# A third k-tile pair in seven-product form in block 2's first FFN product, and two of eight pairs in block 1's gate/up products

## The chip, the core and the metric

The kernel runs on one core of a Trainium2 chip. The metric is the device time of one execution in microseconds (us). Before the change three runs took 2608.23, 2606.01 and 2612.13 us; their median is 2608.23.

## The reference, cut to what matters

Two transformer blocks follow each other on 256 tokens of width 2048, all in float32. The change touches one product of each.

```python
# block 1, w_ffn_in: 2048 x 11264, FFN_HIDDEN = 5632
h = rms_norm(x, ffn_pre_g[l])
gate, up = jnp.split(h @ w_ffn_in[l], 2, axis=-1)
x = x + rms_norm((jax.nn.silu(gate) * up) @ w_ffn_out[l], ffn_post_g[l])
...
# block 2, w_ff1: 2048 x 8192
f = jnp.square(jax.nn.relu(x @ w_ff1[layer])) @ w_ff2[layer]
x = layer_norm(DEEPNORM_ALPHA * x + f, ln_ff_g[layer], ln_ff_b[layer])
```

## The kernel before, in words

**Split operands.** Each float32 operand is split into a high part `h` (a rounded copy, ScalarE, L233) and a low part `l` (operand minus `h`, VectorE, L234). A product is three matmuls on TensorE: high by high, high by low, low by high. The tokens stay as the stationary operand (two blocks of 128 tokens, `tb` 0 and 1); the weights move, 512 columns at a time, and each result of 128 tokens x 512 columns fills one PSUM bank.

**The weight stream.** `Stream` loads the weights from HBM in the order of use, in halves of 128 x 1024 (512 KB) on SyncE's queue, into five buffers. Each half becomes one unit (`h` and `l`, five buffers of each). `half()` (L265) hands out a unit and splits ahead until four later units are issued; a unit's split can start only when TensorE is done with the unit five places earlier.

**Normal and seven-product pairs.** k runs over 16 tiles of 128, taken as eight pairs. For 256 tokens x 1024 columns a normal pair (N in `SEQ`) costs two halves, each used by 12 matmuls: 24 matmuls. In seven-product form (S; Strassen's scheme in Winograd's variant) the pair is a 2 x 2 block product: two k-tiles, two token blocks, two column blocks of 512. Seven products instead of eight, so 21 matmuls. VectorE forms the sums of the weights from the two raw halves `a` and `b`: `s` (L254, L255) and `t` (L257, L258), and `splitting4` (L240) makes four units of them, used by 6, 6, 6 and 3 matmuls. The sums of the tokens are formed once by `seven_gen` (L548) and lie in the tile `seven`.

**`seven` (L569).** It runs the eight pairs for one group of 1024 columns. The four results are accumulated in `c[tb, nb]`; products that several results share go to four more banks `m[1]`, `m[5]`, `m[6]`, `m[7]`, over all S pairs of the group. After the last S pair VectorE combines the `m` (L622 to L628, ScalarE copies one, L621), and after the last pair it adds the `c` (L632). With four `c` and four `m`, all eight PSUM banks are in use: the pool `pa` has three, `pb` five.

**Block 2's FFN (`ff2`, L1886)** works the 8192 hidden columns in eight parts of 1024: `i0 i1 o0 i2 o1 ...` (`FF_ORDER`), where `i` is the first product and `o` the second. `i0` is in plain form by `rowsmm` (L457); `i1` to `i7` call `seven` with `SEQ = "NSNNSNNN"`, two S pairs of eight. **Block 1's FFN (`ffn`, L1648)** works 5632 hidden columns in parts of 8, 8, 8, 8, 4 and 8 tiles of 128; all its gate/up products (`i0` to `i5`) are plain `rowsmm`: 512 gate columns, then the 512 up columns that belong to them, evacuated by `ev_glu` (L1677: ScalarE applies Silu, VectorE multiplies).

**What sets the order.** Each engine's program is in the order in which this code emits it. Work that follows a product is pushed with `later` and emitted by `settle`, one step after each half. So a finished 128 x 512 block of hidden values is transposed on TensorE (four 128 x 128 transposes into a bank of `pb`, L1701 in `turn_later`), and one step later the result is split out of PSUM (ScalarE L642, then VectorE L643). Before the first S pair of a group, `seven` empties that list (`while self.late: self.settle()`) and only then takes the four `m` banks, since no bank is left for a transpose.

Of the kernel before, what the change touches and what calls it, by code (L numbers as in the profile page):

```python
# [11 lines left out]
F32R = mybir.dt.float32r  # L12
# [3 lines left out]
AF = mybir.ActivationFunctionType  # L16
# [6 lines left out]
S = 256  # L23
# [15 lines left out]
SEQ = "NSNNSNNN"  # L39
# [21 lines left out]
def _seven(w):  # L61


    u = []
    for p, s in enumerate(SEQ):
        t = w[256 * p:256 * p + 256].reshape(2, 128, 2, 512)
        if s == "N":
            u.append(t.transpose(1, 2, 0, 3).reshape(128, 2048))
        else:
            u.append(np.stack([t[0, :, 1], t[0, :, 0], t[1, :, 0], t[1, :, 1]], axis=1).reshape(128, 2048))  # L70
    return np.stack(u)


def _fours():

    parts = [16 * i for i, s in enumerate(FF_ORDER) if s[0] == "i" and s != "i0"]
    return [i + 2 * p - 16 * len(FF_ORDER) for i in parts for p, s in enumerate(SEQ) if s == "S"]


def _weights(a):  # L80
# [15 lines left out]
    for step in FFN_ORDER:  # L96
        p = int(step[1:])
        lo, hi = int(starts[p]), int(starts[p + 1])
        u.append(gate_up[lo // 4:hi // 4].reshape(-1, 128, 2048) if step[0] == "i" else _rows(w_fo[lo * 128:hi * 128]))
# [11 lines left out]
    for step in FF_ORDER:  # L111
        p = int(step[1:])
        lo, hi = int(starts[p]), int(starts[p + 1])
        if step[0] == "o":
            u.append(_rows(w2[lo * 128:hi * 128]))
        else:
            u.append((_seven if p else _rows)(w1[:, lo * 128:hi * 128]))
# [57 lines left out]
class Stream:  # L175
# [64 lines left out]
    def splitting4(self, j, raw, part):  # L240


        nc = self.nc
        h, l = (self.hp.tile([128, 1024], F32R, tag=x, name=f"{x}{j}") for x in ("h", "l"))
        if part == 0:
            a, b = self.loaded.pop(raw), self.loaded.pop(raw + 1)
            s, t = self.t4([128, 1024], "s"), self.t4([128, 1024], "t")
            self.four = a, b, s, t
        a, b, s, t = self.four
        lo, hi = slice(0, 512), slice(512, 1024)  # L250
        v, n = (b, s, t, a[:, hi])[part], 512 if part == 3 else 1024
        nc.scalar.activation(out=h[:, :n], in_=v, func=AF.Copy)
        if part == 0:
            nc.vector.tensor_tensor(s[:, lo], a[:, hi], a[:, lo], OP.subtract)  # L254
# [4 lines left out]
        nc.vector.tensor_tensor(l[:, :n], v, h[:, :n].bitcast(F32), OP.subtract)  # L259
        if part == 3:  # L260
            self.four = None
        self.done[j] = (h, l)
        self.ns += 1
# [40 lines left out]
class Prog:  # L304
# [152 lines left out]
    def rowsmm(self, xp, nkt, ncb, evac, chain=None, lead=7, lag=0, begin=None):  # L457
# [15 lines left out]
        def run(cb, k2, hl, tb, part=(0, 1)):  # L473
            two = chain and (cb, tb) == (ncb - 1, 1)
            if k2 == 0 and part[0] == 0:
                ps[cb, tb] = (self.acc(), self.bank()) if two else (self.acc(),)
# [71 lines left out]
    def seven_gen(self, xp, box):  # L548
# [3 lines left out]
        ps = [p for p, s in enumerate(SEQ) if s == "S"]  # L552
        t = self.slot([128, len(ps), 2, 4, 128], "seven", F32R)
        for i, p in enumerate(ps):
            yield 1.9
            w = self.t4([128, 2, 4, 128], "s7")
# [9 lines left out]
            self.split2(s, t[:, i, 0], t[:, i, 1])  # L566
        box.append(t)

    def seven(self, xp, st, out, own, more):  # L569
# [4 lines left out]
        last = len(SEQ) - 1  # L574
        last_s = SEQ.rindex("S")
# [15 lines left out]
        for p, s in enumerate(SEQ):  # L591
# [13 lines left out]
            sum_ = lambda i: (st[:, si, 0, i], st[:, si, 1, i])  # L605
# [1042 lines left out]
    def ffn(self):  # L1648
# [6 lines left out]
        ss = self.cp.tile([128, 2, 8], F32, tag="ss", name="ss2")  # L1655
        last = len(FFN_PARTS) - 1
        for step in FFN_ORDER:
            p = int(step[1:])
            nt = FFN_PARTS[p]
            if step[0] == "i":  # L1660
                hid[p] = Pair(self, "hid", nt)
                self.rowsmm(hT, 16, nt // 2, self.ev_glu(hid[p]), lag=4 if p == 0 else 0)
                continue
# [11 lines left out]
            self.rowsmm(hid.pop(p), nt, 4, ev)  # L1675
# [210 lines left out]
    def ff2(self):  # L1886
# [6 lines left out]
        for step in FF_ORDER:  # L1893
            p = int(step[1:])
            nt = FF_PARTS[p]
            if step[0] == "i":
# [11 lines left out]
                if p == 0:  # L1908
                    self.rowsmm(hT, 16, nt // 4, ev, lag=4, begin=lambda: sg.append(self.start(self.seven_gen(hT, st))))
                    continue  # L1910
# [9 lines left out]
                self.seven(hT, st[0], relu2, [self.bank] * 4, [self.acc] * 3 + [self.bank])  # L1920
# [79 lines left out]
```

## Time and profile before

| | |
|---|---|
| median of three runs | 2608.23 us |
| the profiled execution | 2606.45 us, span 2604.7 us |
| TensorE busy / weight load | 99% / 84% of the span |
| VectorE busy | 63% |
| ScalarE busy | 49% |
| granted TensorE clock, mean | 0.996 |
| HBM | 188 GB/s over the span |

Busy time of TensorE is that of overlapping matmuls: a matmul is shown from its start to its modelled end, and the next one starts before that end. The distance of two starts is the time that one more matmul takes. In a row of the timeline the columns are start (us), duration (us), engine, line, operation, output and inputs; a bracket holds the idle time before it and what ended it. In a row of a group, after the bar, stand total busy time (us), mean duration (ns) and the idle time of the engine just before.

### The profile page before, as it was taken

How to read it: one execution, taken by the hardware profiler on the slowest of the kernel's cores; microseconds unless marked ns; L12 is line 12 of the kernel's file. 1: busy time of each engine (PE TensorE's matmuls, PEld its weight loads, DVE VectorE, ACT ScalarE, POOL GpSimd, SP SyncE). 2: the span in 40 equal slices, each digit the busy share in tenths (PEclk: the TensorE clock that was granted, in tenths of full speed). 3: DMA queues.
4: the chain of work that ended last, by engine and by line, in shares of the span. 5: the costliest groups of instructions: out<-in, count | busy, mean ns of one | idle time of the engine just before them, and what ended most of it. 6: DMA issues, size and time to landing. Idle time of an engine off the chain costs nothing. (4 is left out here: it accounts for less than half of the span.)

```text
span 2604.7 us, 33758 instructions
## 1 busy us (share of the span) xinstructions
PE 2574.6 (99%) x13011; PEld 2183.2 (84%) x13011; DVE 1634.4 (63%) x2069; ACT 1281.0 (49%) x1715; POOL 62.4 (2%) x59
## 2 busy tenths in 40 slices
PE   9999999999999999999999999999999999999998
PEld 8999888988888888888888888888788888888886
DVE  5776857766454555554676774456676666676666
ACT  6544666655444444434444464444455545554553
POOL 0000000110000000000010000000100000000001
PEclk9999999999999999999999999999999999999999
DMA  7544557545555555555555655565455555656563
GB/s 282 178 156 146 178 178 244 195 168 187 194 186 194 187 193 188 193 193 190 183 184 188 206 178 179 193 224 185 150 186 198 196 195 179 200 196 209 193 204 121
DMA packets 134081, 493.33 MB, mean 189 GB/s; under 512 B 15149, under 2 KB 15541, under 8 KB 131744
## 3 DMA queue, kind: packets, MB, share of 16 engines
q1 hardware_dynamic: 129888, 470.34, 54.6%
q0 software_dynamic: 2880, 17.76, 2.1%
q10 hardware_dynamic: 1152, 3.07, 0.3%
q8 instruction: 102, 1.67, 0.3%
q14 instruction: 59, 0.48, 0.1%
HBM read 486.91 MB, written 2.11 MB: 188 GB/s over the span
## 5 line engine op out<-in xcount | busy, mean ns | idle before, releaser
L234 DVE TENSOR_TENSOR l<-w,h 128x1024 fp32r<-128x1024 f32 (+1 forms) x852 | 1038.0, 1223 | 857.1 <-ACT h L233 852.5
L233 ACT ACTIVATE h<-w 128x1024 fp32r<-128x1024 f32 (+1 forms) x855 | 898.6, 1057 | 913.0 <-PE pa L488 715.4
L486 PE MATMUL pa<-h,hid 128*128 128x512 f32 (+1 forms) x864 | 338.5, 392 | 0.0
L488 PE MATMUL pa<-h,hid 128*128 128x512 f32 (+1 forms) x864 | 335.0, 388 | 0.0
L487 PE MATMUL pa<-l,hid 128*128 128x512 f32 (+1 forms) x864 | 334.4, 387 | 0.0
L487 PE MATMUL pa<-l,hT 128*128 128x512 f32 x748 | 291.7, 390 | 2.3 <-DVE l L234 2.3
L486 PE MATMUL pa<-h,hT 128*128 128x512 f32 x748 | 293.4, 392 | 0.0
L488 PE MATMUL pa<-h,hT 128*128 128x512 f32 x748 | 291.7, 390 | 0.0
L486 PE MATMUL pa<-h,xT 128*128 128x512 f32 x500 | 201.0, 402 | 2.5 <-ACT ghg L912 1.3
L488 PE MATMUL pa<-h,xT 128*128 128x512 f32 x500 | 195.3, 391 | 0.0
L487 PE MATMUL pa<-l,xT 128*128 128x512 f32 x500 | 194.9, 390 | 0.0
L488 PEld LDWEIGHTS pa<-h,hid 128*128 128x128 f32 x864 | 162.2, 188 | 33.7
L487 PEld LDWEIGHTS pa<-l,hid 128*128 128x128 f32 x864 | 162.4, 188 | 32.2
L486 PEld LDWEIGHTS pa<-h,hid 128*128 128x128 f32 x864 | 162.3, 188 | 31.8
L487 PEld LDWEIGHTS pa<-l,hT 128*128 128x128 f32 x748 | 140.8, 188 | 31.6 <-DVE l L234 2.9
L488 PEld LDWEIGHTS pa<-h,hT 128*128 128x128 f32 x748 | 140.7, 188 | 29.4
L486 PEld LDWEIGHTS pa<-h,hT 128*128 128x128 f32 x748 | 140.7, 188 | 28.6
L583 PE MATMUL pb<-h,hT 128*128 128x512 f32 x378 | 147.1, 389 | 0.0
L585 PE MATMUL pb<-h,hT 128*128 128x512 f32 x378 | 147.1, 389 | 0.0
L584 PE MATMUL pb<-l,hT 128*128 128x512 f32 x378 | 147.0, 389 | 0.0
L443 PE MATMUL pa<-xT,h 128*128 128x256 f32 x496 | 143.2, 289 | 2.3 <-ACT xT L662 2.3
L444 PE MATMUL pa<-xT,h 128*128 128x256 f32 x496 | 141.3, 285 | 0.0
(493 smaller groups left out, 3971.3 us busy)
## 6 DMA issues: line engine op xcount, KB each, us to landing
w<-W SPq DMA_DIRECT2D x889, 512.0 KB, 3.3
row<-rows POOLq DMA_DIRECT2D x7, 1024.0 KB, 7.3
xn<-x ACTq DMA_DIRECT2D x2, 1024.0 KB, 10.2
mn<-mem POOLq DMA_DIRECT2D x2, 1024.0 KB, 7.4
memraw<-memT POOLq DMA_DIRECT2D x2, 1024.0 KB, 6.7
x<-x POOLq DMA_DIRECT2D x2, 1024.0 KB, 7.5
xraw<-xT SPq DMA_DIRECT2D x3, 512.0 KB, 9.8
out<-x SPq DMA_DIRECT2D x6, 256.0 KB, 2.5
```

The lines of the kernel that those rows point to most:

```text
L233: nc.scalar.activation(out=h[:, s], in_=t[:, s], func=AF.Copy)
L234: (nc.gpsimd if j in self.slow else nc.vector).tensor_tensor(l[:, s], t[:, s], h[:, s].bitcast(F32), OP.subtract)
L443: mm(o, h[:, k], xp.H(kt), start=kt == 0, stop=False)
L444: mm(o, h[:, k], xp.L(kt), start=False, stop=False)
L486: mm(o, xh, h[:, k, c], start=kt == 0, stop=False)
L487: mm(o, xh, l[:, k, c], start=False, stop=False)
L488: mm(o, xl, h[:, k, c], start=False, stop=kt == nkt - 1)
L583: mm(o, ah, wh, start=first, stop=False)
L584: mm(o, ah, wl, start=False, stop=False)
L585: mm(o, al, wh, start=False, stop=end)
```

## The change

Block 2's `i1` to `i7` use `SEQ_FF = "NSNSNSNN"`: three S pairs instead of two. Block 1's `i1` to `i5` are computed by `seven` too, with `SEQ_GLU = "NSNNSNNN"`: for each 512 gate columns and the 512 up columns that belong to them one call, nb = 0 being gate and nb = 1 up; two calls in parts of eight tiles, one in the part of four, nine in all. A second call of a part takes its banks the other way round (`swap`): `c` in three banks of `pa` and one of `pb`, `m` in four of `pb`, and the `o` part behind it starts in `pb`. The new `glu` does what `ev_glu` did, from SBUF. The order inside an S pair changes: `m[1]` comes first and `c[0,0]` last, with the weights laid out for it, and `s` is one VectorE operation on 1024 columns with a repeated operand, where two worked on 512 each. `seven_gen` now also runs in block 1's `i0`, and makes its tile for two pairs at a time.

```diff
-SEQ = "NSNNSNNN"
+SEQ_GLU = "NSNNSNNN"
+SEQ_FF = "NSNSNSNN"
...
-            u.append(np.stack([t[0, :, 1], t[0, :, 0], t[1, :, 0], t[1, :, 1]], axis=1).reshape(128, 2048))
+            u.append(np.stack([t[0, :, 0], t[1, :, 1], t[0, :, 1], t[1, :, 0]], axis=1).reshape(128, 2048))
...
-        v, n = (b, s, t, a[:, hi])[part], 512 if part == 3 else 1024
+        v, n = (a, s, t, b[:, hi])[part], 512 if part == 3 else 1024
         nc.scalar.activation(out=h[:, :n], in_=v, func=AF.Copy)
         if part == 0:
-            nc.vector.tensor_tensor(s[:, lo], a[:, hi], a[:, lo], OP.subtract)
-            nc.vector.tensor_tensor(s[:, hi], b[:, hi], a[:, lo], OP.subtract)
+            two = lambda v: v.rearrange("p (i c) -> p i c", i=2)
+            nc.vector.tensor_tensor(two(s), two(a), b[:, lo][:, None].to_broadcast([128, 2, 512]), OP.subtract)
         if part == 1:
-            nc.vector.tensor_tensor(t[:, lo], b[:, hi], s[:, lo], OP.add)
-            nc.vector.tensor_tensor(t[:, hi], b[:, lo], t[:, lo], OP.subtract)
+            nc.vector.tensor_tensor(t[:, lo], a[:, hi], s[:, lo], OP.add)
+            nc.vector.tensor_tensor(t[:, hi], b[:, hi], t[:, lo], OP.subtract)
...
+        own, more = [self.bank] * 4, [self.acc] * 3 + [self.bank]
+        if swap:
+            own, more = more, own
         c = {(tb, nb): own[2 * tb + nb]() for tb in range(2) for nb in range(2)}
...
-            for pair in (((c[0, 0], tok(k0 + 1, 0)), (c[0, 1], sum_(3))), ((m[5], sum_(0)), (m[7], sum_(2))),
-                         ((m[6], sum_(1)), (c[1, 0], tok(k0 + 1, 1))), ((m[1], tok(k0, 0)),)):
+            for pair in (((m[1], tok(k0, 0)), (c[0, 1], sum_(3))), ((m[5], sum_(0)), (m[7], sum_(2))),
+                         ((m[6], sum_(1)), (c[1, 0], tok(k0 + 1, 1))), ((c[0, 0], tok(k0 + 1, 0)),)):
...
-                self.rowsmm(hT, 16, nt // 2, self.ev_glu(hid[p]), lag=4 if p == 0 else 0)
+                if p == 0:
+                    self.rowsmm(hT, 16, nt // 2, self.ev_glu(hid[p]), lag=4, begin=lambda: sv.append(self.start(self.seven_gen(hT, SEQ_GLU, st))))
+                    continue
+                self.drain(sv[0])
+                for b in range(nt // 4):
+                    self.seven(hT, SEQ_GLU, st, self.glu(hid[p], b), swap=b % 2 == 1)
+                after_swap = nt == 8
...
+    def glu(self, hp, b):
...
+        def out(i, tb, nb, t):
+            r = self.rxx[:, tb:tb + 1]
+
+            def f():
+                if nb == 0:
+                    sg[tb] = t
+                    nc.scalar.activation(out=t, in_=t, func=AF.Silu, scale=r)
+                    return
+                nc.vector.scalar_tensor_tensor(out=t, in0=t, scalar=r, in1=sg[tb], op0=OP.mult, op1=OP.mult)
+                self.turn_later(t, hp, 4 * b, tb)
+            self.wait_later(i // 2, f)
```

Three places show what this does to the engines' programs. The first is TensorE at the first S pair of block 2's `i1`. Before, two transposes of `i0`'s last hidden values (`sq` into banks of `pb`) are followed by `c[0,0]` (pb_858) and `c[0,1]` (pb_859):

```order
L1701 MATMUL pb_862_16138<-ident_258,sq_854_16094 128x128 [waits DVE_49,PE_49]
L1701 MATMUL pb_862_16138<-ident_258,sq_854_16094 128x128 x3
L1701 MATMUL pb_863_16145<-ident_258,sq_855_16096 128x128 [waits DVE_49]
L1701 MATMUL pb_863_16145<-ident_258,sq_855_16096 128x128 x3
L583 MATMUL pb_858_16100<-h652_16056,hT20_798_14975 128x512 [waits Activation_49]
L584 MATMUL pb_858_16100<-l652_16057,hT20_798_14975 128x512
L585 MATMUL pb_858_16100<-h652_16056,hT20_798_14975 128x512
L583 MATMUL pb_859_16101<-h652_16056,seven_843_15835 128x512
```

In the change the same place reads as follows, with `m[1]` (pb_962) first:

```order
L1750 MATMUL pb_957_16478<-ident_258,sq_949_16434 128x128 [waits DVE_49,PE_49]
L1750 MATMUL pb_957_16478<-ident_258,sq_949_16434 128x128 x3
L1750 MATMUL pb_958_16485<-ident_258,sq_950_16436 128x128 [waits DVE_49]
L1750 MATMUL pb_958_16485<-ident_258,sq_950_16436 128x128 x3
L606 MATMUL pb_962_16495<-h688_16395,hT20_891_15307 128x512 [waits DVE_49]
L607 MATMUL pb_962_16495<-l688_16396,hT20_891_15307 128x512
L608 MATMUL pb_962_16495<-h688_16395,hT20_891_15307 128x512
L606 MATMUL pb_954_16441<-h688_16395,seven_936_16185 128x512
```

The matmul behind the transposes now waits for VectorE: `m[1]` takes the one bank of `pb` that the second transpose has just filled, the other four being held by `c`. Before, `m[1]` took that bank as well, but was the last of the pair's seven products.

The second place is TensorE between the first and the second 512 gate columns of block 1's `i1`. Before, the second transpose (`sg_440`) stands one half, 12 matmuls, behind the first, ahead of the next half of a plain product:

```order
L486 MATMUL pa_444_6931<-h225_6864,hT0_374_5644 128x512
L487 MATMUL pa_444_6931<-l225_6865,hT0_374_5644 128x512
L488 MATMUL pa_444_6931<-h225_6864,hT0_374_5644 128x512
L1701 MATMUL pb_446_6963<-ident_258,sg_440_6768 128x128 [waits DVE_49]
L1701 MATMUL pb_446_6963<-ident_258,sg_440_6768 128x128 x3
L486 MATMUL pa_443_6924<-h226_6882,hT4_375_5645 128x512 [waits Activation_49]
```

In the change both transposes stand together after the second call's first N pair, and its first S pair follows:

```order
L608 MATMUL pb_461_6972<-h229_6910,hT0_374_5644 128x512
L1750 MATMUL pb_462_7007<-ident_258,u4_454_6847 128x128 [waits DVE_49]
L1750 MATMUL pb_462_7007<-ident_258,u4_454_6847 128x128 x3
L1750 MATMUL pb_463_7016<-ident_258,u5_455_6848 128x128 [waits DVE_49]
L1750 MATMUL pb_463_7016<-ident_258,u5_455_6848 128x128 x3
L606 MATMUL pb_467_7026<-h230_6928,hT0_374_5644 128x512 [waits Activation_49]
L607 MATMUL pb_467_7026<-l230_6929,hT0_374_5644 128x512
L608 MATMUL pb_467_7026<-h230_6928,hT0_374_5644 128x512
L606 MATMUL pa_459_6970<-h230_6928,seven_421_6086 128x512
```

Here `m[1]` (pb_467) waits for its weights alone; it takes a bank that an addition on `c` has freed. The banks of the two transposes go to `m[7]` and `m[6]`, a few products later.

The third place is VectorE at the second S pair of a part of block 2. Before, the four units of the pair have two operations for `s`, two for `t` and four for `l`:

```order
L254 TENSOR_TENSOR s_898_16880<-w690_16831 128x512
L255 TENSOR_TENSOR s_898_16880<-w691_16843,w690_16831 128x512
L259 TENSOR_TENSOR l696_16879<-w691_16843,h696_16878 128x1024
L257 TENSOR_TENSOR t_899_16881<-w691_16843,s_898_16880 128x512
L258 TENSOR_TENSOR t_899_16881<-w691_16843,t_899_16881 128x512
L259 TENSOR_TENSOR l697_16899<-s_898_16880,h697_16898 128x1024
L259 TENSOR_TENSOR l698_16917<-t_899_16881,h698_16916 128x1024
L259 TENSOR_TENSOR l699_16933<-w690_16831,h699_16932 128x512
```

In the change `s` is one operation, and two plain units later the next S pair begins:

```order
L279 TENSOR_TENSOR l732_17206<-w688_17094,h732_17205 128x1024
L277 TENSOR_TENSOR t_996_17208<-w688_17094,s_995_17207 128x512
L278 TENSOR_TENSOR t_996_17208<-w689_17177,t_996_17208 128x512
L279 TENSOR_TENSOR l733_17219<-s_995_17207,h733_17218 128x1024
L279 TENSOR_TENSOR l734_17228<-t_996_17208,h734_17227 128x1024
L279 TENSOR_TENSOR l735_17244<-w689_17177,h735_17243 128x512
L254 TENSOR_TENSOR l736_17264<-w690_17179,h736_17263 128x1024
L254 TENSOR_TENSOR l737_17276<-w691_17191,h737_17275 128x1024
L275 TENSOR_TENSOR s_997_17289<-w692_17203,w693_17259 128x1024
```

Between two S pairs VectorE now has two plain units (l736, l737) where it had four.

More of the change, by code (lines that the diff above doesn't have):

```diff
@@ L69, in _seven @@
         else:
[L70 removed]
+            u.append(np.stack([t[0, :, 0], t[1, :, 1], t[0, :, 1], t[1, :, 0]], axis=1).reshape(128, 2048))
     return np.stack(u)
 def _fours():
[L76 to L77 removed]
+    at = lambda i, seq: [i + 2 * p for p, s in enumerate(seq) if s == "S"]
+    u, n = [], 0
+    for step in FFN_ORDER:
+        nt = FFN_PARTS[int(step[1:])]
+        if step[0] == "i" and step != "i0":
+            for b in range(nt // 4):
+                u += at(n + 16 * b, SEQ_GLU)
+        n += 4 * nt if step[0] == "i" else 2 * nt
+    n += MID
+    for step in FF_ORDER:
+        if step[0] == "i" and step != "i0":
+            u += at(n, SEQ_FF)
+        n += 16
+    return [i - n for i in u]
 def _weights(a):
@@ L98, in _weights @@
         lo, hi = int(starts[p]), int(starts[p + 1])
-        u.append(gate_up[lo // 4:hi // 4].reshape(-1, 128, 2048) if step[0] == "i" else _rows(w_fo[lo * 128:hi * 128]))
+        if step[0] == "o":
+            u.append(_rows(w_fo[lo * 128:hi * 128]))
+        elif p == 0:
+            u.append(gate_up[lo // 4:hi // 4].reshape(-1, 128, 2048))
+        else:
+            for b in range(lo * 128, hi * 128, 512):
+                u.append(_seven(np.concatenate([w_fi[:, i + b:i + b + 512] for i in (0, FFN)], axis=1), SEQ_GLU))
     u += [
@@ L455, in cols, with rowsmm @@
         assert not held
-    def rowsmm(self, xp, nkt, ncb, evac, chain=None, lead=7, lag=0, begin=None):
+    def rowsmm(self, xp, nkt, ncb, evac, chain=None, lead=7, lag=0, begin=None, swap=False):
         mm = self.nc.tensor.matmul
@@ L475, in run @@
             if k2 == 0 and part[0] == 0:
-                ps[cb, tb] = (self.acc(), self.bank()) if two else (self.acc(),)
+                ps[cb, tb] = (self.acc(), self.bank()) if two else ((self.bank if swap and cb == 0 else self.acc)(),)
             h, l = hl
@@ L546, in rowsmm, with seven_gen @@
             chain.after[tb]()
-    def seven_gen(self, xp, box):
+    def seven_gen(self, xp, seq, st):
         nc = self.nc
-        ps = [p for p, s in enumerate(SEQ) if s == "S"]
-        t = self.slot([128, len(ps), 2, 4, 128], "seven", F32R)
-        for i, p in enumerate(ps):
+        for i, p in enumerate(p for p, s in enumerate(seq) if s == "S"):
             yield 1.9
+            if i % 2 == 0:
+                t = self.slot([128, 2, 2, 4, 128], "seven", F32R)
             w = self.t4([128, 2, 4, 128], "s7")
@@ L565, in seven_gen, with seven @@
             yield 0.7
-            self.split2(s, t[:, i, 0], t[:, i, 1])
-        box.append(t)
-    def seven(self, xp, st, out, own, more):
+            self.split2(s, t[:, i % 2, 0], t[:, i % 2, 1])
+            st.append(t[:, i % 2])
+    def seven(self, xp, seq, st, out, swap=False):
         nc, mm, stream = self.nc, self.nc.tensor.matmul, self.stream
-        last = len(SEQ) - 1
-        last_s = SEQ.rindex("S")
+        last = len(seq) - 1
+        last_s = seq.rindex("S")
+        own, more = [self.bank] * 4, [self.acc] * 3 + [self.bank]
+        if swap:
+            own, more = more, own
         c = {(tb, nb): own[2 * tb + nb]() for tb in range(2) for nb in range(2)}
@@ L590, in seven @@
         si = 0
-        for p, s in enumerate(SEQ):
+        for p, s in enumerate(seq):
             if s == "N":
@@ L1674, in ev @@
                     nc.vector.tensor_tensor(c, ps, c, OP.add)
-            self.rowsmm(hid.pop(p), nt, 4, ev)
+            self.rowsmm(hid.pop(p), nt, 4, ev, swap=after_swap)
+            after_swap = False
+    def glu(self, hp, b):
+        nc = self.nc
+        sg = {}
+        def out(i, tb, nb, t):
[8 more added lines that the diff above has]
+            self.wait_later(i // 2, f)
+        return out
     def ev_glu(self, hp):
@@ L1908, in ff2 @@
                 if p == 0:
-                    self.rowsmm(hT, 16, nt // 4, ev, lag=4, begin=lambda: sg.append(self.start(self.seven_gen(hT, st))))
+                    self.rowsmm(hT, 16, nt // 4, ev, lag=4, begin=lambda: sg.append(self.start(self.seven_gen(hT, SEQ_FF, st))))
                     continue
@@ L1918, in relu2 @@
                     self.wait_later(i, f)
-                self.seven(hT, st[0], relu2, [self.bank] * 4, [self.acc] * 3 + [self.bank])
+                self.seven(hT, SEQ_FF, st, relu2)
                 continue
```

11 lines of the change are left out of this document (7 added, 4 removed).

## The prediction

> **What bounds the kernel now.** I read the page's busy shares first, then the list of what TensorE waited for, then the timeline of TensorE in the stages that the change touches.
>
> ```profile
> PE 2574.6 (99%) x13011; PEld 2183.2 (84%) x13011; DVE 1634.4 (63%) x2069; ACT 1281.0 (49%) x1715; POOL 62.4 (2%) x59
> ```
>
> ```profile
> PE pb L1392 <- DVE x L1354: 2.7, 2, 2.0
> ...
> PE pb L1701 <- DVE hid L643: 1.4, 1, 1.4
> ...
> PE pa L486 <- ACT ga L1851: 0.3, 1, 0.3
> ```
>
> The second view (columns: total us, times, longest) has eleven rows in all; they add up to 17.0 us of 2604.7. Only one of them lies in a stage that is changed, the 1.4 us at L1701. So TensorE's own work sets the time, and a matmul taken out is worth the distance to the next one:
>
> ```profile
> 1965.21 0.39 PE L583 MATMUL pb<-h,hT 128*128 128x512 f32 x1
> ...
> 1976.77 0.39 PE L486 MATMUL pa<-h,hid 128*128 128x512 f32 x1
> ```
>
> 51 matmuls start from the first row up to the last: 11.56 us / 51 = **0.2267 us each**. The 0.39 us in the rows is a duration with the next matmul inside it, and is no price.
>
> **The change, part by part.** *Matmuls removed.* An S pair has 21 matmuls where an N pair has 24. Block 2 gets one more S pair in each of seven parts; block 1 gets two in each of nine calls. That is 7 + 18 = 25 pairs and 75 matmuls; the rows of TensorE's program fall by 75 (12236 to 12161), and the transposes stay. 75 x 0.2267 = **17.0 us less**. All 75 lie on the engine that sets the end, in stages where it is never idle but for the one row above. The Trainium skill ("Trainium Kernel Development and Optimization", Performance Expectations) says that matmul busy time is a bad metric because matmuls are pipelined; the rows agree, with 0.39 against 0.2267. By the 0.39 the saving would be 29.2 us.
>
> *The first S pair of block 2's `i1`.* Here the trace has its 1.4 us:
>
> ```profile
> 1937.51 0.60 PE L1701 MATMUL pb<-ident,sq 128*128 128x128 f32 x4
> 1938.14 0.60 ACT L642 ACTIVATE hid<-pb 128x512 fp32r<-128x512 f32 x1 [2.48 <-PE pb L1701]
> 1938.78 0.69 DVE L643 TENSOR_TENSOR hid<-pb,hid 128x512 fp32r<-128x512 f32 x1 [1.90 <-ACT hid L642]
> 1939.52 0.66 PE L1701 MATMUL pb<-ident,sq 128*128 128x128 f32 x4 [1.41 <-DVE hid L643]
> 1939.93 0.48 PE L583 MATMUL pb<-h,hT 128*128 128x512 f32 x1
> 1940.21 0.60 ACT L642 ACTIVATE hid<-pb 128x512 fp32r<-128x512 f32 x1 [1.47 <-PE pb L1701]
> 1940.85 0.69 DVE L643 TENSOR_TENSOR hid<-pb,hid 128x512 fp32r<-128x512 f32 x1 [1.38 <-ACT hid L642]
> ```
>
> The second transpose waits until the first one's bank has been read twice (1.41 us). That stays. But now the matmul behind it is `m[1]`, which takes the second one's bank, so it too waits for the ScalarE copy and the VectorE subtraction: until 1940.85 + 0.69 + 0.05 (the 0.05 from 1939.47 to 1939.52) = 1941.59 in place of 1939.93. That is **1.66 us more**. Queued behind it on TensorE is the whole S pair; VectorE was idle before both rows of L643, so nothing delays the release further.
>
> *The first S pair of block 1's `i1`.* By the order, the same three events stand there in one bank of `pb`: transpose, transpose, `m[1]`. The two transposes stand 12 matmuls apart (2.72 us), and the first one's read-out (0.60 + 0.69 us behind it, with the 0.69 us of the fourth unit's `l` ahead of it on VectorE) fits between them. The second is followed by `m[1]` at once: by the same rows **1.66 us** again. Sum of the two: 3.3 us. Bounds: 0 if the release were seen at once, 2 x 2.1 us if a 0.4 us operation stands ahead each time.
>
> *The four second calls (`swap`).* The second call's S pair follows 24 matmuls, 5.44 us, behind the end of the first call, and has to find both hidden blocks ready for the transposes. VectorE's queue from that end on, with durations from these groups:
>
> ```profile
> L632 DVE TENSOR_TENSOR u<-pb,u 128x512 f32<-128x512 f32 x28 | 17.3, 681 | 0.0
> L234 DVE TENSOR_TENSOR l<-w,h 128x1024 fp32r<-128x1024 f32 (+1 forms) x852 | 1038.0, 1223 | 857.1 <-ACT h L233 852.5
> L1692 DVE SCALAR_TENSOR_TENSOR sg<-pa,rxx,sg 128x512 f32<-128x512 f32 x22 | 15.4, 743 | 0.0
> L1689 ACT ACTIVATE sg<-pa,rxx 128x512 f32<-128x512 f32 x22 | 15.1, 690 | 9.7 <-PE pa L488 9.7
> ```
>
> four additions (back to back 2.48 us in the trace at 1976.49, where they begin 0.28 us ahead of the next product), the third unit's `l` (1.22), the first multiply (0.74), the fourth unit's `l` (0.69), the second multiply (0.74): 5.87 us, so it ends some 5.6 us behind the end of the call. The Silus (0.69) and copies on ScalarE run beside it. The first transpose needs the first multiply, ready at 4.2; the second starts 0.35 us behind the first, at 5.8. It fits by about 0.2 us, so I take **0**. The banks of the transposes go to `m[7]` and `m[6]`, 9 and 12 matmuls (2.0 and 2.7 us) behind the second transpose, and the two read-outs on VectorE (2 x 0.69) end about 0.7 us ahead of either. Bounds: nothing, and 4 x 1.66 = 6.6 us if VectorE is a microsecond later than this.
>
> *VectorE and ScalarE in the denser pattern.* What one S pair costs VectorE is in these rows:
>
> ```profile
> 1946.57 0.69 DVE L254 TENSOR_TENSOR s<-w 128x512 f32<-128x512 f32 x1
> ...
> 1950.36 1.22 DVE L259 TENSOR_TENSOR l<-s,h 128x1024 fp32r<-128x1024 f32 x1
> ...
> 1953.88 0.69 DVE L259 TENSOR_TENSOR l<-w,h 128x512 fp32r<-128x512 f32 x1 [1.01 <-ACT h L252]
> ```
>
> ```profile
> 1957.05 0.39 PE L583 MATMUL pa<-h,seven 128*128 128x512 f32 x1
> ```
>
> Three `l` of 1.22, one of 0.69, two `t` of 0.69 and `s` at 1.22 (one operation on 1024 columns, taken as the other 1024-column ones; no row has the repeated operand) make 6.9 us; a normal pair is 2 x 1.22 = 2.4 us. In `NSNSNS` VectorE needs 9.4 us for each 45 matmuls, 10.2 us of TensorE: 92%. It keeps up, though by little. A unit also has time in hand: the second unit's `l` above ends at 1951.58 and is used at 1957.05. With two plain units between S pairs instead of four, the units' buffers, freed by TensorE, put every split about 2.5 us or more ahead of its use. So I take **0**; if `s` cost 2.4 us, a period would be 10.6 us and the lag over three pairs 1.2 us, still inside that. ScalarE needs 3 x 1.06 + 0.63 for an S pair and 2 x 1.06 for a normal one, 5.9 of 10.2 us. The rest of VectorE's new work (the additions and multiplies of nine calls, the token sums of `seven_gen` in `i0`) lies in plain stretches, where L234 has 857 us of idle time ahead of it. The Trainium skill ("VectorE: DVE Perf Modes", the errata on SBUF-source operations) gives (N+151)/0.96 ns for an fp32 `tensor_tensor`, an estimate of 1.22 us for `s`; no run here shows it with a repeated operand, and the sum would be the same.
>
> *Transfers.* The bytes are the same. The first raw half of an S pair is now free after the second unit, not the fourth, so the load that reuses its buffer starts earlier; the 7.3 us that ScalarE spends waiting for loads ahead of S pairs now
>
> ```profile
> L252 ACT ACTIVATE h<-w 128x1024 fp32r<-128x1024 f32 (+1 forms) x28 | 23.7, 847 | 40.6 <-PE pb L585 20.5 <-PE pa L488 11.6 <-DMA w<-W 7.3
> ```
>
> are hidden from TensorE, and should stay so: **0**.
>
> **Sum.** -17.0 + 1.66 + 1.66 = **-13.7 us**. The profiled execution took 2606.45 us, so one like it would take 2592.8. It lies 1.8 us below the median of the three runs, 2608.23; on the median the forecast is **2594.5 us**.
>
> **The rivals.** *The banks at the four second calls are late* (VectorE a microsecond behind my queue): +6.6, so -7.1 and 2601.1 us. For it: that queue fits by 0.2 us at the second transpose and by 0.7 us at `m[7]`. Against it: the additions may start before the last matmul of the call, as they did at 1976.49. Chance 0.12.
>
> *The clock falls.* The program's start shows that idle time can cost speed:
>
> ```profile
> 10.45 0.50 PE L443 MATMUL pa<-xT,h 128*128 128x256 f32 x1 [2.27 <-ACT xT L662]
> ...
> 11.57 0.41 PE L443 MATMUL pa<-xT,h 128*128 128x256 f32 x1
> ...
> 13.70 0.41 PE L444 MATMUL pa<-xT,h 128*128 128x256 f32 x1
> ...
> 14.24 0.28 PE L444 MATMUL pa<-xT,h 128*128 128x256 f32 x1
> 14.36 0.28 PE L445 MATMUL pa<-xT,l 128*128 128x256 f32 x1
> ```
>
> ```profile
> 10.00:15.00 5.00, 4.53 (x23) 0.66 1.03 420
> 1930.00:1945.00 15.00, 13.59 (x64) 1.00 0.27 85
> ```
>
> After 2.27 us idle the distance was 0.213 us (ten matmuls from 11.57 to 13.70) instead of 0.12 for some 15 matmuls, 1.4 us lost, with a mean granted clock of 0.66 (the number behind the busy time). The single 1.41 us at 1939 left it at 1.00. In the change, 1.41 and 1.66 us stand 0.41 us apart in block 2's `i1`. If they together do what 2.27 us did, 1.4 us are added: -12.3, 2595.9 us. Chance 0.15. The Trainium skill ("TensorE: Matmul & The Clock Gate", Part 1) states the rule as half speed after an idle window of about 3.4 us; by it neither place needs to trip, and the 2.27 us in the trace were enough.
>
> *VectorE becomes the bound in `NSNSNSNN`.* The place is the three S pairs of block 2's seven parts, the price whatever an S pair takes beyond its share. It decides once a pair needs 7.75 us (10.2 - 2.45) plus a third of the 2.5 us in hand, about 8.6 us; from there each further microsecond costs 3 x 7 = 21 us. The saving would be gone at 9.2 us, 2.3 us above my count; with a repeated operand that made `s` cost 4 us it would be 9.7, and the time 13.7 - 21 x 1.1 = 9 us above before, 2617 us. For it: 92% of VectorE. Against it: six of the pair's seven operations have rows. Chance 0.04, most of it slower.
>
> *The change does not do what it says.* The order shows 75 matmuls fewer, and no other engine's program gets longer than its idle time, so I give this 0.02, at no change.
>
> **How the numbers follow.** Forecast 2594.5 us with 0.67; with the clock case, which lies in its own spread, 0.82; then 0.12 for 2601.1, 0.04 and 0.02. The range takes in the bounds: below, no new wait and a run like the fastest, 2606.0 - 17.0 = 2589; above, the late banks and two microseconds of the runs' spread, 2603. About 0.2% (5.2 us) is what a measurement of this kernel can tell from no change. Faster by more than that 0.93, within it 0.04, slower 0.03.
>
> **What would show it.** In the changed profile a part of block 2 is shorter by 3 matmuls. These two rows from the chain of waits, one part apart, give 87.59 us now and should give 86.91:
>
> ```profile
> 1982.38 0.44 PE pb L1701 x4
> 2069.97 0.44 PE pb L1701 x4
> ```
>
> ```profile
> L1674 DVE TENSOR_TENSOR yf<-pa,yf x32: 679/681/684, 907.7 to 1272.1; 128x512 f32<-128x512 f32 x32
> ```
>
> Block 1's additions to `yf`, from the first at 907.7 to the last at 1272.1 us (the last columns of the row), span two parts of eight and one of four: 30 matmuls, 6.8 us less. What TensorE waits for should have the 1.4 us again and two new entries of about 1.7 us for VectorE's L666, one in each block; more of them, some 1.7 us at each second call of block 1, would be the late banks. Waits for an `l` inside S pairs of block 2 would be VectorE's limit, and my 0 for it wrong. A distance other than 0.2267 us, or a clock below 1.00 behind block 2's two waits, would change the first term or add the 1.4 us.

## The result, and the profile after

Four runs of the changed kernel took 2594.06, 2594.27, 2594.29 and 2596.54 us, median **2594.28 us**. The kernel before took 2605.14 to 2612.13 us beside it (four runs, median 2607.12). The ratio is **0.995, 95% interval 0.9933 to 0.9967**: faster by half a per cent. The profiled execution is the slowest of the four, 2596.54 us with a span of 2594.8.

The page's busy shares, then the list of what TensorE waited for (total us, times, longest):

```profile
PE 2561.9 (99%) x12936; PEld 2171.5 (84%) x12936; DVE 1786.2 (69%) x2270; ACT 1325.9 (51%) x1777; POOL 62.4 (2%) x59
```

```profile
PE pb L606 <- DVE hid L666: 2.8, 2, 1.4
...
PE pb L1750 <- DVE hid L666: 1.4, 1, 1.4
```

TensorE has 75 matmuls fewer (13011 before), VectorE 201 operations more, and TensorE's share is still 99%. The old wait of the second transpose is there (L1750), and the two new ones are matmuls of `seven` (L606) that wait for VectorE's read-out at L666, one in each block. No S pair waits for an `l`, and no second call waits for a bank.

The timeline of TensorE, ScalarE and VectorE in block 2's `i1` (start, duration, engine and line; the bracket holds the idle time ahead):

```profile
1929.12 0.60 PE L1750 MATMUL pb<-ident,sq 128*128 128x128 f32 x4
...
1931.13 0.66 PE L1750 MATMUL pb<-ident,sq 128*128 128x128 f32 x4 [1.41 <-DVE hid L666]
1931.83 0.60 ACT L665 ACTIVATE hid<-pb 128x512 fp32r<-128x512 f32 x1 [1.47 <-PE pb L1750]
1932.46 0.69 DVE L666 TENSOR_TENSOR hid<-pb,hid 128x512 fp32r<-128x512 f32 x1 [1.38 <-ACT hid L665]
1933.20 0.50 PE L606 MATMUL pb<-h,hT 128*128 128x512 f32 x1 [1.41 <-DVE hid L666]
...
1933.85 0.63 PE L608 MATMUL pb<-h,hT 128*128 128x512 f32 x1
...
1936.83 0.51 PE L606 MATMUL pa<-h,seven 128*128 128x512 f32 x1
...
1937.40 0.39 PE L608 MATMUL pa<-h,seven 128*128 128x512 f32 x1
```

`m[1]` starts 2.07 us behind the second transpose (1931.13 to 1933.20); before, the same step took 0.41 us. That is the 1.66 us of the forecast. The rows below it are what the sum of the forecast put at nothing: from 1933.85 to 1936.83 seven matmuls take 2.98 us, 0.426 us each, where 0.2267 is the rule. The windows there (length, then busy us and number for TensorE, its weight loads, VectorE, ScalarE and GpSimd; then the granted clock, the DMA share and GB/s):

```profile
1930.20:1933.61 3.41, 1.06 (x6) 0.79 (x7) 1.59 (x3) 1.70 (x3) 0.00 (x0) 1.00 0.30 109
1933.61:1937.02 3.41, 3.41 (x10) 2.63 (x9) 1.11 (x2) 1.06 (x1) 0.00 (x0) 0.51 0.36 137
1937.02:1940.43 3.41, 3.41 (x17) 2.83 (x16) 3.41 (x4) 2.09 (x2) 0.00 (x0) 0.99 0.37 129
```

The granted clock is halved for 3.41 us, right behind 3.41 us in which TensorE was busy for 1.06 us: ten matmuls where seventeen follow. In block 1's `i1` there is a wait of the same size, and the clock over 680 to 690 us stays at 1.00:

```profile
683.04 0.60 PE L1750 MATMUL pb<-ident,sg 128*128 128x128 f32 x4
...
685.05 0.50 PE L606 MATMUL pb<-h,hT 128*128 128x512 f32 x1 [1.41 <-DVE hid L666]
```

The other places that the forecast named, in the chain of waits (one part of block 2 apart) and in the rows of block 1's additions:

```profile
1976.56 0.44 PE pb L1750 x4
...
2063.47 0.44 PE pb L1750 x4
```

```profile
L1704 DVE TENSOR_TENSOR yf<-pa,yf x26: 679/683/684, 917.1 to 1263.7; 128x512 f32<-128x512 f32 x26
L1704 DVE TENSOR_TENSOR yf<-pb,yf x6: 681/684/684, 905.8 to 1247.1; 128x512 f32<-128x512 f32 x6
```

A part of block 2 takes 86.91 us (87.59 before), exactly three matmuls less; the additions span 905.8 to 1263.7, 357.9 us, where 364.4 - 6.8 = 357.6 was forecast.

So by its parts the change is worth -17.0 + 1.66 + 1.66 + 1.6 = **-12.1 us**. The medians are 12.8 us apart, with an interval of 8.6 to 17.5 us: the times alone can't tell -12.1 from the forecast's -13.7. Taken from the profiled execution of before, 2606.45, the -12.1 gives 2594.3, where three of the four runs lie. The fourth, the profiled one, has two more falls of the clock far ahead of the changed stages,

```profile
170.00:175.00 5.00, 5.00 (x20) 3.63 (x20) 1.23 (x2) 1.58 (x2) 0.00 (x0) 0.74 0.24 75
235.00:240.00 5.00, 5.00 (x35) 5.00 (x35) 1.77 (x3) 0.00 (x0) 0.00 (x0) 0.72 0.53 190
```

each about 3.4 us at half speed or some 1.7 us lost, while the profile of before has one at 10 to 15 us that this one lacks. That is 1.7 us of the 2.2 between -12.1 and the difference of the two profiled executions, -9.9; 0.5 us were not traced.

### The profile page after: what moved, and what is told of

Its sections match the earlier page's. It is cut to its first block, busy times and chain, and to the rows that moved or that the text cites. A ratio compares the mean times of both kernels' runs of the same rounds, so it can differ in the third digit from the quotient of the medians.

```text
span 2594.8 us, 33924 instructions
## 1 busy us (share of the span) xinstructions
PE 2561.9 (99%) x12936; PEld 2171.5 (84%) x12936; DVE 1786.2 (69%) x2270; ACT 1325.9 (51%) x1777; POOL 62.4 (2%) x59
## 3 DMA queue, kind: packets, MB, share of 16 engines
q8 instruction: 101, 1.65, 0.3%
## 5 line engine op out<-in xcount | busy, mean ns | idle before, releaser
L254 DVE TENSOR_TENSOR l<-w,h 128x1024 fp32r<-128x1024 f32 (+1 forms) x802 | 975.3, 1223 | 669.6 <-ACT h L253 659.0
L253 ACT ACTIVATE h<-w 128x1024 fp32r<-128x1024 f32 (+1 forms) x805 | 844.9, 1058 | 752.0 <-PE pa L508 442.0
L506 PE MATMUL pa<-h,hid 128*128 128x512 f32 (+1 forms) x808 | 316.4, 392 | 0.0
L508 PE MATMUL pa<-h,hid 128*128 128x512 f32 (+1 forms) x808 | 313.1, 388 | 0.0
L606 PE MATMUL pb<-h,hT 128*128 128x512 f32 x669 | 260.9, 390 | 2.8 <-DVE hid L666 2.8
L608 PE MATMUL pb<-h,hT 128*128 128x512 f32 x669 | 260.5, 389 | 0.0
L607 PE MATMUL pb<-l,hT 128*128 128x512 f32 x669 | 260.4, 389 | 0.0
L606 PEld LDWEIGHTS pb<-h,hT 128*128 128x128 f32 x669 | 125.6, 188 | 28.9 <-DVE hid L666 3.3
L608 PEld LDWEIGHTS pb<-h,hT 128*128 128x128 f32 x669 | 125.6, 188 | 26.2
L607 PEld LDWEIGHTS pb<-l,hT 128*128 128x128 f32 x669 | 125.6, 188 | 25.9
L465 PE MATMUL pa<-xT,l 128*128 128x256 f32 x496 | 141.2, 285 | 1.0 <-DVE l L254 1.0
L459 PE MATMUL pa<-xT,h 128*128 128x512 f32 x384 | 134.0, 398 | 0.0
L506 PEld LDWEIGHTS pa<-h,xT 128*128 128x128 f32 x500 | 94.4, 189 | 25.3 <-issue 2.7
```

Of the source, the lines that this page charges most:

```text
L253: nc.scalar.activation(out=h[:, s], in_=t[:, s], func=AF.Copy)
L254: (nc.gpsimd if j in self.slow else nc.vector).tensor_tensor(l[:, s], t[:, s], h[:, s].bitcast(F32), OP.subtract)
L459: mm(o, h[:, k], xp.both(kt), start=kt == 0, stop=kt == nkt - 1)
L465: mm(o, l[:, k], xp.H(kt), start=False, stop=kt == nkt - 1)
L506: mm(o, xh, h[:, k, c], start=kt == 0, stop=False)
L508: mm(o, xl, h[:, k, c], start=False, stop=kt == nkt - 1)
```

## The experiments

All times are medians beside runs of the kernel before on the same chip, or one execution where one is named. Two theories stand against each other first: A, that block 2's two waits bring the low clock with them; B, the sum as forecast, with the low clock an accident.

**Each block's part alone.** For the first, block 1's gate/up products go back to plain form; for the second, block 2 goes back to two S pairs.

```diff
...
-                for b in range(nt // 4):
-                    self.seven(hT, SEQ_GLU, st, self.glu(hid[p], b), swap=b % 2 == 1)
...
+                self.rowsmm(hT, 16, nt // 2, self.ev_glu(hid[p]), lag=4 if p == 0 else 0)
```

```diff
-SEQ_FF = "NSNSNSNN"
+SEQ_FF = "NSNNSNNN"
```

> Only block 2's part of the change: three S pairs in its parts, block 1's gate/up products plain as before. Theory A (the sum as the changed kernel's trace now suggests it): 7 pairs x 3 x 0.2267 = -4.8 us, +1.66 us for the first product behind the second transpose, and +1.6 us because TensorE's granted clock falls to 0.50 for some 3.4 us behind that second wait: -1.5 us, 2605 us beside a before of 2606.5. Theory B (the sum on record, where the low clock behind the wait is one of the accidental falls that the same profile also has at 170 and 235 us, with no idle time ahead of them): -3.1 us, 2603.4 us. The two differ by less than the runs spread, so the trace decides: A wants a window of low clock right behind the two waits of block 2's first seven-product part, B none there. Both want 86.91 us for a part of block 2 and no wait in block 1.

Measured: 2608.2 us against 2608.75, ratio 0.9994 (0.9985 to 1.0003). The time can't tell -1.5 from -3.1. The trace can: the clock falls to a mean of 0.66 in a stretch of 5 us behind the second wait of block 2's `i1`, which ends at 1945.85, as A wants; a part takes 86.91 us.

```profile
1945.00:1950.00 5.00, 4.15 (x11) 3.29 (x12) 2.14 (x3) 2.08 (x3) 0.00 (x0) 0.66 0.33 104
```

> Only block 1's part of the change: two S pairs in nine gate/up calls, block 2 back at two S pairs, but with the new order of products inside a pair. Theory A: 18 x 3 x 0.2267 = -12.2 us, +1.66 us at block 1's first call, +1.66 us at block 2's first part (the new order is still there) and +1.6 us of low clock behind it: -7.3 us, 2599.1 us. Theory B, without the clock: -8.9 us, 2597.6 us. A rival for the size of the saving: if a matmul were worth its 0.39 us of busy time, -21 us and about 2589 us. Expected in the trace: the additions to yf span 357.6 us as in the whole change, a part of block 2 is back at 87.59 us, and no wait stands at the four second calls.

Measured: 2602.94 us against 2608.75, ratio 0.9971 (0.9959 to 0.9983), -5.8 us; A's -7.3 and B's -8.9 both lie inside, the -21 of the busy time does not (the interval ends at -10.7). Block 1's additions span 903.4 to 1261.2 us, 357.8. In block 2's `i1` the timeline has these two rows, the first transpose there and the first one behind the part:

```profile
1926.65 0.60 PE L1750 MATMUL pb<-ident,sq 128*128 128x128 f32 x4
...
1974.64 0.60 PE L1750 MATMUL pb<-ident,u 128*128 128x128 f32 x4
```

They are 47.99 us apart. Before, the same two stood 44.71 us apart (1937.51, quoted with the prediction, to 1982.22), with the same number of matmuls. So 3.28 us are added in this one place by the new order of products, twice the forecast's 1.66. This interval is the yardstick of the next two experiments.

**Another bank, and a filled wait.** In the first, `m[6]` takes the transposes' bank in calls without `swap`. In the second, seven matmuls of zeros are put into the new wait of block 2, in `m[5]`'s bank; they are thrown away.

```diff
-                m = {i: f() for i, f in zip((5, 7, 6, 1), more)}
+                m = {i: f() for i, f in zip((5, 7, 6, 1) if swap else (1, 5, 7, 6), more)}
```

```diff
...
                 m = {i: f() for i, f in zip((5, 7, 6, 1), more)}
+                if fill:
+                    for _ in range(fill):
+                        mm(m[5], self.junk[:, :128], self.junk, start=True, stop=True)
...
-                self.seven(hT, SEQ_FF, st, relu2)
+                self.seven(hT, SEQ_FF, st, relu2, fill=7 if p == 1 else 0)
```

> The whole change, but in the calls that keep their sums in the five banks the product used fifth, m[6], takes the bank of the two transposes, and m[1], used first, takes one of the other three. The second transpose's read-out then has 12 matmuls (2.7 us) for its 1.66 us. Theory A: both new waits go (2 x 1.66 us), and the clock stays at 1.00 behind the one wait of 1.41 us that is left, 1.6 us more: 4.9 us below the changed kernel, 2589.4 us. Theory B (the clock's fall was an accident): 3.3 us below, 2591 us. Rival C: the wait only moves on to m[6] or to the sums that release banks later: no gain, 2594.3 us.

Measured: 2588.79 us (2587.64 to 2593.57) against 2608.75, ratio 0.9925 (0.9912 to 0.9937). A expected 2589.4. The timeline of TensorE, and the window around it:

```profile
1923.62 0.60 PE L1750 MATMUL pb<-ident,sq 128*128 128x128 f32 x4
...
1925.63 0.66 PE L1750 MATMUL pb<-ident,sq 128*128 128x128 f32 x4 [1.41 <-DVE hid L666]
...
1926.05 0.48 PE L606 MATMUL pa<-h,hT 128*128 128x512 f32 x1
...
1967.65 0.60 PE L1750 MATMUL pb<-ident,u 128*128 128x128 f32 x4
```

```profile
1920.00:1935.00 15.00, 13.59 (x64) 11.12 (x63) 11.43 (x13) 6.89 (x9) 0.00 (x0) 1.00 0.37 114
```

`m[1]` follows the second transpose after 0.42 us again, now in a bank of `pa`; the clock stays at 1.00 behind the one wait that is left. The interval is 44.03 us: 44.71 less three matmuls and nothing else. The wait of `m[1]` in block 1 is gone as well: TensorE's list names L666 once, for the 1.4 us at L1750. Nothing moved on to `m[6]`: rival C falls.

> The whole change, and in block 2's first seven-product part seven matmuls of zeros into m[5]'s bank between the second transpose and the first product; they are thrown away, since m[5]'s own first matmul starts it anew. They need 7 x 0.2267 = 1.59 us and lie in the second wait, which is 1.66 us long, so the wait itself costs what it did. Theory A (idle time is what lowers the clock): the clock stays at 1.00 behind it and 1.6 us come back, 2592.7 us. Theory B (an accident, or something that the transposes bring with them): nothing changes, 2594.3 us, and in the trace the clock is as low as before or 1.00 for no reason of this edit. If the seven take longer than the wait, up to 0.3 us more.

The timeline of TensorE, and two windows around it:

```profile
1930.88 0.66 PE L1753 MATMUL pb<-ident,sq 128*128 128x128 f32 x4 [1.41 <-DVE hid L669]
...
1931.59 1.46 PE L630 MATMUL pa<-junk 128*128 128x512 bf16 x6
...
1932.95 0.50 PE L606 MATMUL pb<-h,hT 128*128 128x512 f32 x1
...
1974.57 0.60 PE L1753 MATMUL pb<-ident,u 128*128 128x128 f32 x4
```

```profile
1925.00:1940.00 15.00, 13.54 (x63) 10.43 (x63) 9.81 (x12) 6.13 (x8) 0.00 (x0) 1.00 0.33 106
1929.96:1933.37 3.41, 2.43 (x12) 1.45 (x14) 1.60 (x3) 1.69 (x3) 0.00 (x0) 1.00 0.28 111
```

`m[1]` starts 2.07 us behind the second transpose, as late as in the changed kernel (the row of the zeros shows six of the seven), but the clock is 1.00. With the first transpose at 1928.88 the interval is 45.69 us. That puts three kernels with the same products in a row: 44.03 without the wait, 45.69 with the wait filled, 47.27 with the wait left idle (1929.12 to 1976.39 in the changed kernel). **The wait costs 1.66 us and the idleness in it another 1.58.** The median, 2594.63 us (2592.26 to 2597.67), does not show the 1.6 us; falls of the clock elsewhere differ from run to run by more (this profile has two at 10 to 20 us).

So A holds: in all nine profiles that have the two idle waits in a row (the changed kernel twice, either block's part alone, and the five variants below that keep them) the clock falls behind them; in none of the four without (the kernel before, these two variants and the last one below) does it. In all nine the fall starts 0.23 to 0.85 us behind the start of `m[1]`, and the 3.41 us ahead of it hold 0.89 to 1.51 us of TensorE's work; in the filled wait the 3.41 us up to the same place hold 2.43 us (the second of the two rows above). A stretch of 3.41 us that ends in the middle of the two waits was not met. The Trainium skill ("TensorE: Matmul & The Clock Gate", Part 1) has the clock follow TensorE's activity in windows of 3413 ns that run free of the kernel's own times, and a fall after an idle window. The length agrees with the 3.41 us here, and so do windows that run free (the grid in the last section); a whole window without work was not needed, 1.06 us of work out of 3.41 was too little. Part 4 adds that transposes don't count as work in the same way; 0.66 of those 1.06 us are transposes, and no run here tells the two apart.

**How far VectorE is from its limit.** The same subtraction for `s` is made once more, then twice more, in block 2's S pairs; then the three S pairs stand side by side.

```diff
+            self.at4 = raw
...
-            nc.vector.tensor_tensor(two(s), two(a), b[:, lo][:, None].to_broadcast([128, 2, 512]), OP.subtract)
+            for _ in range(1 + 1 if self.at4 >= self.halves - 256 else 1):
+                nc.vector.tensor_tensor(two(s), two(a), b[:, lo][:, None].to_broadcast([128, 2, 512]), OP.subtract)
```

```diff
-SEQ_FF = "NSNSNSNN"
+SEQ_FF = "NSSSNNNN"
```

> The whole change, with the subtraction that makes s done twice in each seven-product pair of block 2 (the same values written again, all on VectorE): 1.22 us more for each of 21 pairs, 8.1 us for a pair. By the rule on record (a pair decides from 8.6 us on) nothing, 0 us. By the changed kernel's trace every l is ready 2.1 us or more ahead of its first matmul; a period of 45 matmuls would need 9.4 + 1.2 = 10.6 of 10.2 us, so the lead falls to 0.9, 0.5 and 0.1 us behind the three pairs: 0 to 2 us in all. A rival by which VectorE were already the bound: 21 x 1.22 = 26 us more.

Measured, one execution: 2594.24 us, no wait for an `l` in block 2's pairs, a part still 86.91 us. Nothing, as by the rule, and within the 0 to 2 us of the leads.

> The same with that subtraction done three times, 2.44 us more for a pair, 9.3 us. By the rule on record, (9.3 - 8.6) x 21 = 15 us more. By the leads in the changed kernel's trace, 2.1 - 2.4 = -0.3 us behind the first pair and 1.6 us more behind each of the other two: 3.5 us a part, 24 us, less what the plain units between them give back; so 10 to 24 us, with TensorE waiting for l behind the seven-product pairs of all seven parts. If VectorE had room that I don't see, 0.

Measured, one execution: 2598.93 us. From what TensorE waited for, and from the timeline (the same transpose one part apart):

```profile
PE pa L609 <- DVE l L281: 3.1, 6, 0.5
```

```profile
2061.53 0.60 PE L1752 MATMUL pb<-ident,u 128*128 128x128 f32 x4
...
2149.26 0.60 PE L1752 MATMUL pb<-ident,u 128*128 128x128 f32 x4
```

A part takes 87.73 us, 0.82 more. There are six waits, one in each part from `i2` to `i7`, and none in `i1`: 4.9 us, not 10 to 24. VectorE does become the bound, but later than I had it. The lead that I took for VectorE's own is in these rows of the changed kernel, behind a part's first S pair:

```profile
2108.98 1.06 ACT L253 ACTIVATE h<-w 128x1024 fp32r<-128x1024 f32 x1 [2.09 <-PE pb L608]
...
2110.07 2.59 DVE L254 TENSOR_TENSOR l<-w,h 128x1024 fp32r<-128x1024 f32 x2 [2.45 <-ACT h L253]
```

```profile
2113.49 0.39 PE L606 MATMUL pb<-h,hT 128*128 128x512 f32 x1
```

The first of the two `l` ends at some 2111.3 and its unit is used from 2113.49 on: 2.2 us of lead. But VectorE stood idle for 2.45 us ahead of it, for a copy by ScalarE that itself waited 2.09 us for TensorE to free a buffer (the first row). So the lead is set by the buffers; VectorE's own reserve is the idle time on top of it.

> The whole change with the same 21 seven-product pairs of block 2 side by side (pairs 1, 2 and 3 of a part instead of 1, 3 and 5): the same matmuls, the same work on VectorE, another order. If VectorE's lead decides: each pair behind the first takes 6.9 - 4.76 = 2.1 us more of VectorE than of TensorE, and the lead of 2.1 us behind the first becomes -2.2 us behind the third: 2.2 us a part, some 15 us more, with waits for l. If only the number of operations counts, as in the busy shares, nothing: 2594 us. By the sum on record the order of the pairs has no price of its own.

Measured, one execution: 2601.47 us.

```profile
PE pa L607 <- DVE l L279: 3.0, 6, 0.7
```

Six parts take 87.65 to 87.96 us, 0.7 to 1.1 us more each, with the same matmuls and the same operations on VectorE. So the order does have a price, a third to a half of the 2.2 us a part that I expected, by the same misreading of the lead. That only the count of operations matters falls.

**The banks at the second calls.** Two more operations on VectorE ahead of a multiply of `glu`:

```diff
+                if tb == 0 and b % 2 == 1:
+                    for _ in range(2):
+                        nc.vector.scalar_tensor_tensor(out=self.junk, in0=t, scalar=r, in1=sg[tb], op0=OP.mult, op1=OP.mult)
                 nc.vector.scalar_tensor_tensor(out=t, in0=t, scalar=r, in1=sg[tb], op0=OP.mult, op1=OP.mult)
```

> The whole change, with two more operations on VectorE (a 128x512 multiply whose result is thrown away, 0.75 us each) ahead of the first multiply of each of the four second calls of block 1. In the changed kernel's trace the second multiply of the call at 721 us ends at 727.2, and the second transpose could start at 727.7; the last read-out ends at 730.0, and m[7] starts at 730.3. By the price on record (nothing up to 0.2 us, then the delay itself, up to 1.66 us a call) the 1.5 us push the second transpose back by 1.0 to 1.3 us: four waits, 4 to 5 us in all, with the first transpose or the read-outs named as releasers. If the banks have more time than that, 0.

Measured, one execution: 2595.75 us, no wait. But the operations were in the wrong place: a call's multiplies are emitted during the call behind it, so `b % 2 == 1` put them behind the second calls. This run says nothing on the question. With `b % 2 == 0`:

> The experiment on the late banks with its two extra operations (1.5 us of VectorE) now where the second calls run: ahead of the first multiply of a first call, which VectorE does during the second call's first matmuls. In the changed kernel's trace, in the call at 721 us, the first multiply ends at 725.9 and its transpose starts at 727.3; the second ends at 727.2 and its transpose could start at 727.7. With 1.5 us more they end at 727.4 and 728.7: waits of 0.1 and 1.0 us, some 1.1 us at each of four calls, 4 to 5 us in all (by the price on record 1.5 - 0.2 = 1.3 us a call, 5.2 us). If the second calls have more time than the queue on record gave them, 0.

Measured, one execution: 2600.71 us. From what TensorE waited for, and the timeline of the call:

```profile
PE pb L1753 <- DVE u L1724: 2.4, 4, 0.6
```

```profile
728.55 0.66 PE L1753 MATMUL pb<-ident,u 128*128 128x128 f32 x4
...
729.82 0.66 PE L1753 MATMUL pb<-ident,u 128*128 128x128 f32 x4 [0.61 <-DVE u L1724]
```

Four waits, one at each second call, with the multiply as releaser. The second transpose starts 1.27 us behind the first, where 0.35 is the distance without a wait: 0.9 us, and the first is itself about 0.2 us late. That is 1.1 us a call, as expected from the leads, and block 1's additions, whose span holds two second calls, take 360.4 us in place of 357.9. The rival was real, with its point of decision about 0.4 us beyond VectorE's queue.

**The version that the experiments point to.** The bank order of above, and in block 2's `i1` two sums and `m[1]` in `pa`, so that each transpose finds a free bank:

```diff
...
+        if first:
+            own, more = [self.acc] * 2 + [self.bank] * 2, [self.acc] + [self.bank] * 3
...
-                m = {i: f() for i, f in zip((5, 7, 6, 1), more)}
+                m = {i: f() for i, f in zip((5, 7, 6, 1) if swap else (1, 5, 7, 6), more)}
...
-                self.seven(hT, SEQ_FF, st, relu2)
+                self.seven(hT, SEQ_FF, st, relu2, first=p == 1)
```

> The bank order of the earlier experiment in all calls, and in block 2's first seven-product part two of the four sums and m[1] in the three accumulator banks, so that the two transposes find a free bank each: the old wait of 1.41 us (1.65 us between starts) goes as well. If nothing else waits for the accumulators of the part before, 1.65 us below that experiment, 2587.1 us, and 20 us below before. A rival: the accumulators are read later than the five banks, and c[0,1] waits for them instead: no gain, 2588.8 us.

Measured: **2586.99 us** (2586.57 to 2591.71) against 2606.69, ratio 0.9927 (0.9915 to 0.994).

```profile
1924.44 1.03 PE L1752 MATMUL pb<-ident,sq 128*128 128x128 f32 x8
...
1966.82 0.60 PE L1752 MATMUL pb<-ident,u 128*128 128x128 f32 x4
```

Both transposes run in one go, nothing waits there, and the interval is 42.38 us, 1.65 below the earlier bank order. It beats both kernels; the changed kernel, run beside it on the same chip, is the next entry.

> The changed kernel once more, beside the other runs on this chip. By the parts measured in the traces (75 x 0.2267 = 17.0 us less, two waits of 1.66 us, 1.6 us of low clock behind block 2's): -12.1 us against before. By the sum on record: -13.7 us. By what the first comparison measured: -12.8 us. The low clock behind block 2's two waits should be there again in the profile.

Measured: 2596.0 us (2593.62 to 2599.64) against 2606.69, ratio 0.9956 (0.9942 to 0.9969), -10.7 us. The interval holds all three sums. In its profile the clock falls behind block 2's waits again, and again at 172 and 240 us.

## Why the prediction was right, and where not

- **-17.0 us for 75 matmuls: right, as far as the traces reach.** Where nothing else changes, 3 matmuls are 0.68 us: 87.59 to 86.91 for a part, 44.71 to 44.03 in the interval without the new wait. Block 1's additions came 6.5 us closer together, where 30 matmuls are 6.8. The 0.39 us of the busy rows would have been wrong by 12 us.
- **+1.66 us in block 2's `i1`: right** to the hundredth (1931.13 to 1933.20 less 0.41), and shown as that: another bank takes it away.
- **+1.66 us in block 1's `i1`: right** (683.04 to 685.05, less the 0.36 us from a transpose to the next start). That the clock would hold there was implied; it did.
- **No price for the clock behind block 2's two waits: wrong.** This is the step that failed. The forecast saw the mechanism, priced it at 1.4 us as a rival and gave it 0.15, because 1.41 us alone had left the clock at 1.00. It should have put the two waits together: with 0.4 us between them, 1.41 and 1.66 us leave about as little work in 3.41 us as the 2.27 us that had made it fall at the start. In the changed kernel it was 1.1 us of work ahead of this fall; in the kernel before, ahead of the fall at 10.57 us, it was 1.14 us:

```profile
7.16:10.57 3.41, 1.14 (x10) 0.94 (x8) 0.87 (x3) 1.31 (x3) 0.00 (x0) 1.00 1.01 392
```

  The fall cost 1.58 us.
- **Nothing for the four second calls: right**, with about 0.4 us to spare; 1.5 us more on VectorE cost 1.1 us a call.
- **Nothing for VectorE in `NSNSNSNN`: right.** `s` with the repeated operand is this group, 1.22 us as taken:

```profile
L275 DVE TENSOR_TENSOR s<-w,w 128x1024 f32<-128x1024 f32 x39 | 47.5, 1219 | 1.1 <-DMA w<-W 1.1
```

  The rival's point of decision, 8.6 us for a pair, was too low: 8.1 us cost nothing and 9.3 us cost 0.82 us a part. By the rival's own slope, three pairs a part, an estimate is 9.3 - 0.27 = 9.0 us. VectorE's idle time ahead of the splits had been left out.
- **Nothing for transfers and ScalarE: not contradicted.** In the changed stages TensorE's list of waits has none for a transfer and one for ScalarE, 0.2 us for a Silu of block 1's `i0` at 612 us, where the token sums are now formed; the kernel before does not have it, and it may be part of the 0.5 us that were not traced. No run varied them alone.
- **The number.** By its parts the forecast should have come out 1.6 us too low. It came out 0.2 us too high, because it put -13.7 on the median of three runs, 1.8 us above the profiled execution. Against that execution the three runs that agree are at -12.2 and the parts say -12.1. The two offsets cancelled: that the number came so close is luck.

## What to carry to other kernels

A small reordering may let one matmul reuse a bank that is still being read out: give the bank of the latest transpose to the sum that is started last, which by the traces was worth 4.9 us here for one line. Add up waits that stand close together before saying what the clock does: each of the two was harmless alone. A lead in front of a use tells an engine's reserve only if that engine was not itself waiting for a buffer.

## What the runs showed of the hardware

The clock's falls come in pieces of 3.41 us at half speed, each worth some 1.6 to 1.7 us, and they do not come in the same places each time. Up to the program's last matmuls, the changed kernel's profile has five:

```profile
172.39:175.80 3.41, 3.41 (x10) 2.64 (x9) 0.48 (x1) 0.00 (x0) 0.00 (x0) 0.50 0.47 154
237.24:240.65 3.41, 3.41 (x18) 3.41 (x18) 0.00 (x0) 0.00 (x0) 0.00 (x0) 0.50 0.46 154
1315.85:1319.26 3.41, 3.41 (x12) 2.72 (x11) 3.41 (x6) 1.72 (x3) 0.00 (x0) 0.50 0.22 52
1879.05:1882.46 3.41, 3.41 (x10) 2.84 (x11) 3.38 (x4) 2.00 (x4) 0.00 (x0) 0.50 0.73 221
1933.66:1937.07 3.41, 3.41 (x10) 2.63 (x9) 1.11 (x2) 1.06 (x1) 0.00 (x0) 0.50 0.37 143
```

Their starts are 19, 316, 165 and 16 times 3.4133 us apart. In each of the thirteen profiles all falls lie on such a grid of windows, and the grid lies elsewhere in each execution: it runs free of the program. Counted in these windows from 15 us on, a full clock fell behind every one that held less than about 1.5 us of TensorE's work, and behind none with more, but for six of another kind. That settles a place where the kernels differ, the waits at block 1's end that every profile has. The first row is the emptiest window there in the changed kernel, whose clock fell behind it at 1315.85; the second is the emptiest in the kernel with the other bank, whose clock held:

```profile
1312.44:1315.85 3.41, 1.45 (x10) 0.98 (x9) 2.58 (x8) 2.72 (x6) 0.00 (x0) 1.00 0.38 152
1307.11:1310.52 3.41, 2.02 (x9) 1.31 (x7) 2.24 (x9) 2.44 (x7) 0.00 (x0) 1.00 0.49 174
```

The six others are the falls at 170 and 235 us, in three of the profiles. They have no idle time ahead of them at all: from 167 to 171 us and from 234 to 237 us TensorE ran matmuls of 64 columns and of 1 column, and the clock fell behind them. The set of falls differs from run to run, and the times go with the clock: of the 16 runs of the kernel before beside the first experiments, the two with a mean granted clock of 0.997 took 2605.7 and 2605.9 us, the six with 0.994 took 2610.5 to 2612.4.
